# Scores of two heads issued in turn into two banks of one PSUM allocation, with the mixers' PSUM as two pairs of banks and one single

## The chip, the cores and the metric

One core of a Trainium2 chip runs the whole program. The metric is the device time of one execution in microseconds, the median of the runs. Lower is better.

## What is computed

One inference step of a two-layer encoder trunk for a prompt of 512 frames and 8 samples of 16 new frames each with 512 cached keys. The first layer mixes with stick-breaking attention (8 heads of 64) beside a gated linear attention (4 heads), the second with softmax attention (16 heads of 64); a SwiGLU feed-forward part follows each. Cut to what the change touches:

```python
# first mixer, attention: strictly causal, keys weighted by a running product
z = einsum('bthd,bshd->bhts', q, k) * 64 ** -0.5
log_keep = where(mask, log_sigmoid(-z), 0.0)
after = reverse cumulative sum of log_keep, without the key itself
o = einsum('bhts,bshd->bthd', where(mask, exp(log_sigmoid(z) + after), 0.0), v)
# second mixer: chunk band, learned bias on clipped relative distance
s = einsum('bthd,bshd->bhts', q, k) * 64 ** -0.5 + rel_table[:, rel]
o = einsum('bhts,bshd->bthd', softmax(where(mask, s, -inf)), v)
```

Outputs are the frames of prompt and samples, and the keys, values and states to be cached, all in float32.

## The kernel before

The kernel is written in a tile language. A scheduler puts each engine's instructions into one fixed order when the program is built, by priorities that the code sets and by its own model of durations; on the chip each engine works through its order, and an instruction waits until what it needs is there. `tile_pool(bufs=n)` is a pool of n buffers: a tile asked for under a tag waits until the last reader of an older tile of that buffer is done.

PSUM has eight banks. Three belong to `pp`, for the projections. The other five are handed out anew in each part: in the first mixer three to `za` and two to `zb`, in the second four and one (`BANKS`), in the feed-forward parts all five to one pool.

Prompt attention works on pairs of heads (p = 0 to 3 in the first mixer, 0 to 7 in the second), whose 64-wide queries and keys lie on partitions 0 to 63 and 64 to 127 of `qT` and `kT`, each as a high and a low part. `attend_prompt` (L426) goes over four blocks b of 128 queries; block b sees n = 128(b+1) keys. For each head it takes a bank `z` from `za`, issues three score matmuls (high by high, high by low, low by high: L436, L437, L438; with the mask of the first mixer a fourth, L440), turns the scores into weights (`stick_break` L400, `softmax` L414: reduction L418, negation L420, exponential L421, reciprocal L422, scaling L423), transposes these in 128-wide pieces into the same bank (L444) and copies them out as `wT` (ScalarE for head 0, L447; VectorE for head 1, L449). Then both heads' value matmuls (L455) go into the first head's bank, and one copy (L457) ends the block.

Around it the projections `proj_ws` (tiles pw, L288 to L290) and `proj_as2` (pm) run from `pp`; after each key projection `evac_k` transposes the keys in `zb` (ktp). The gated linear attention `b_mix` takes its tiles at, og, kv, kvs, at4 and ms from `zb`.

Sample attention (`attend_sample`, L473) handles one sample and eight heads at a time: 8 times in the first mixer, 16 in the second. A bank `z` from `za` holds the scores throughout. For each of four key blocks j the keys are loaded (kr), transposed into a bank kttp (L489; which pool is told by `KTA` and `KTC`, one letter for each j), copied to SBUF (kt; VectorE L492, ScalarE L494) and multiplied (L496). The scores are copied (zsb, L499), made into weights, transposed back into `z` (L508, L510), copied (wTs L509, wT4 L511) and multiplied by the values (L517); the result is copied, transposed and copied once more (L520, L521, L525). Beside the samples run the output projection of the prompt (`out_prompt`, po, L561 to L563) and at the end that of the samples (`out_sample`, ps).

On TensorE a matmul uses the whole array of 128 rows and 128 columns, or a part: the profile writes 64*128 for the scores (64 rows), 128*64 for the values and 128*32 for the samples' products.

Of the kernel before, what the change touches and what calls it, by code (L numbers as in the profile page):

```python
# [8 lines left out]
F32 = mybir.dt.float32  # L9
# [7 lines left out]
P = 128  # L17
# [3 lines left out]
SEQ = 512  # L21
# [25 lines left out]
BANKS = ((3, 2), (4, 1))  # L47
KTA = "bbbb"
KTC = "baba"
# [6 lines left out]
def kernel(  # L56
# [16 lines left out]
    @contextmanager  # L73
    def mixer_pools(na, nb):

        with tc.tile_pool(name="mix", bufs=1, reuse_waits="tile") as m:
            pools["stage"] = m
            with tc.tile_pool(name="pza", bufs=na, space=PSUM, reuse_waits="tile") as a:
                with tc.tile_pool(name="pzb", bufs=nb, space=PSUM, reuse_waits="tile") as b:
                    banks.update(za=a, zb=b)  # L80
                    yield

    @contextmanager
    def ffn_pools():
        with tc.tile_pool(name="ffn", bufs=1, reuse_waits="tile") as m:
            pools["stage"] = m
            with tc.tile_pool(name="pf", bufs=5, space=PSUM, reuse_waits="tile") as a:
                banks.update(za=a, zb=a)
                yield
# [25 lines left out]

    def za(shape, name="za"):
        return banks["za"].tile(shape, F32, tag="za", name=name)
# [308 lines left out]
    def attend_prompt(qT, kT, v, c0, odst, weights, mask):  # L426


        for b in range(4):
            n = (b + 1) * P  # L430
            bs = slice(b * P, n)
            wTs, zs = [], []
            for h in range(2):
                z = za([P, 512], "z")
                r = slice(64 * h, 64 * h + 64)
                MM(z[:, :n], lhsT=qT[r, 0, bs], rhs=kT[r, 0, :n], start=True, stop=False)  # L436
                MM(z[:, :n], lhsT=qT[r, 0, bs], rhs=kT[r, 1, :n], start=False, stop=False)  # L437
                MM(z[:, :n], lhsT=qT[r, 1, bs], rhs=kT[r, 0, :n], start=False, stop=not mask)  # L438
                if mask:
                    MM(z[:, bs], lhsT=identb, rhs=mask_a, start=False, stop=True)  # L440
                w = weights(h, n, z[:, :n])
                wT = vr_([P, b + 1, P], "wT")
                for j in range(b + 1):
                    nc.tensor.transpose(z[:, j * P:(j + 1) * P], w[:, j * P:(j + 1) * P], ident)  # L444
                zv = z[:, :n].rearrange("p (j t) -> p j t", t=P)
                if h == 0:
                    nc.scalar.copy(wT, zv)  # L447
                else:
                    nc.vector.tensor_copy(wT, zv)  # L449
                wTs.append(wT)  # L450
                zs.append(z)
# [21 lines left out]
    def attend_sample(ck, cv, b, cs, qbd, zn, vnew, weights, oS, kttp):  # L473
# [8 lines left out]
        z = za([P, 512], "zs")  # L482
        for j in range(4):
# [3 lines left out]
            tp = (zb if kttp[j] == "b" else za)([P, 4, P], "kttp")  # L487
# [82 lines left out]
    def out_sample(W, x4, gi, hT):  # L570
        ps = [za([P, 512], "ps"), zb([P, 512], "ps")]
# [180 lines left out]
    stack.enter_context(mixer_pools(*BANKS[0]))  # L752
# [60 lines left out]
    def a_sample():  # L813
        with priority(FIRST + 100000):
            zn = new_key_scores(qbd, kfs, msn)
        for b in range(DB):
            with priority(FIRST + 100000 + 1000 * (b + 1)):
                attend_sample(cache_a_k, cache_a_v, b, slice(0, 512), qbd, zn, vt4[:, :512],
                              lambda zs: stick_break(528, zs, zs), oS[:, :4, :], KTA)

# [51 lines left out]
    def b_mix(pr, X0):  # L872
# [47 lines left out]
        kv = [zb([P, 4, P], "kv") for _ in range(2)]  # L920
# [34 lines left out]
        for h in range(2):  # L955
# [4 lines left out]
            at = zb([P, 4, P], "at")  # L960
# [7 lines left out]
            og = zb([P, SEQ], "og")  # L968
# [79 lines left out]
    stack.enter_context(mixer_pools(*BANKS[1]))  # L1048
# [33 lines left out]
    def c_sample(half):  # L1082
# [11 lines left out]
        for b in range(DB):  # L1094
            with priority(p + 1000 * (b + 1)):
                attend_sample(cache_c_k, cache_c_v, b, cs, qbd[half], zn, vt4[:, cs],
                              lambda zs: softmax(528, zs, zs, bsam[:, ::-1]),
                              oS[:, 4 * half:4 * half + 4, :], KTC)
# [69 lines left out]
```

## Time and profile before

| | |
|---|---|
| median of 3 runs | 1821.37 us (1815.55 to 1822.59) |
| profiled execution | 1823.8 us, span 1822.1 us |
| mean granted TensorE clock | 0.969 |
| TensorE, VectorE, ScalarE busy | 1732.9, 1142.8, 833.8 us |
| prompt's scores, first mixer | L436 from 67.1 to 306.6 us |
| prompt's scores, second mixer | L436 from 954.6 to 1199.6 us |

The table of windows gives, for a stretch of the span, the busy time of each engine, the granted clock (1.00 is full speed) and the share of the DMA engines. A row of the timeline is one instruction, or several equal ones merged (x2): start in us, length in us from the first start to the last end, engine, line, operation, tiles, array part, size. Successive matmuls overlap in the pipeline, so that the price of one is the distance between starts, not its length. A row of groups has count, busy us, mean ns of one, and the idle time of the engine before them.

### The profile page before, as it was taken

The numbers are of one execution on the slowest core, as the hardware profiler recorded it, in microseconds if no ns is written. First come the engines' busy times: TensorE is split into PE (matmuls) and PEld (weight loads), VectorE is DVE, ScalarE is ACT, GpSimd is POOL, SyncE is SP. The second block draws the span as 40 slices with busy tenths as digits, with TensorE's granted clock in tenths as the row PEclk, the third lists the DMA queues.
The fourth block names the chain that finished last, engine by engine and source line by source line (L and its number), as shares of the span: only waits on it lengthen the run. The fifth ranks groups of instructions, "written<-read, shape, count | busy, mean of one in ns | idle before, by whom it ended". The sixth has DMA issues, their size and how long they took to land.

```text
span 1822.1 us, 31879 instructions
## 1 busy us (share of the span) xinstructions
PE 1732.9 (95%) x12504; PEld 1550.1 (85%) x12504; DVE 1142.8 (63%) x2285; ACT 833.8 (46%) x1837; POOL 327.7 (18%) x355
## 2 busy tenths in 40 slices
PE   8999998998899999999799999999878999999997
PEld 7898986976898989989698888888757989999896
DVE  5466576767964846747635554665658747658475
ACT  6453444556642534525424333444545525435253
POOL 2000000002513413222200000000104314133130
PEclk9998997998999999999799999999988999999999
DMA  5311222573222232221342223257862222312212
GB/s 141 94 56 47 66 83 95 179 255 105 70 93 70 75 100 63 100 74 66 110 128 77 80 89 95 85 178 263 278 214 65 81 81 72 103 58 93 93 59 81
DMA packets 157430, 192.10 MB, mean 105 GB/s; under 512 B 13232, under 2 KB 109504, under 8 KB 157280
## 3 DMA queue, kind: packets, MB, share of 16 engines
q1 hardware_dynamic: 153696, 178.40, 30.4%
q0 software_dynamic: 3584, 11.67, 2.0%
q8 instruction: 98, 1.61, 0.4%
q14 instruction: 52, 0.43, 0.1%
HBM read 175.75 MB, written 14.29 MB: 104 GB/s over the span
## 4 chain that ended last, share of the span: by engine, by line
PE 80%; DVE 12%; DMA 4%; ACT 2%; issue 2%; SPq 0%; DVEq 0%; ACTq 0%
PE pn L307 6%; PE pn L309 5%; PE pn L308 5%; PE pw L288 5%; PE pw L289 5%; PE pw L290 5%; DVE wl L274 4%; PE px L653 3%; PE px L654 3%; PE px L655 3%; PE z L455 3%; PE py L655 3%; DMA kr<-in_cache_c_k_dram 2%; PE pm L337 2%; PE py L653 2%; PE py L654 2%
## 5 line engine op out<-in xcount | busy, mean ns | idle before, releaser
L274 DVE TENSOR_TENSOR wl<-raw,wh 128x512 fp32r<-128x512 f32 (+1 forms) x350 | 279.3, 807 | 220.8 <-ACT wh L273 218.7
L273 ACT CAST wh<-raw 128x512 fp32r<-128x512 f32 (+1 forms) x350 | 215.4, 618 | 347.3 <-PE pn L309 162.6
L659 POOL TENSOR_TENSOR sw<-raw 128x512 f32<-128x512 f32 x88 | 121.6, 1386 | 498.9 <-DMA raw<-in_w_ffn_gate_dram 292.9
L273 ACT CAST wh<-sw 128x512 fp32r<-128x512 f32 x176 | 109.3, 621 | 177.8 <-PE px L654 78.2
L274 DVE TENSOR_TENSOR wl<-sw,wh 128x512 fp32r<-128x512 f32 x176 | 139.7, 798 | 60.3 <-ACT wh L273 49.1
L308 PE MATMUL pn<-wl,gT 128*128 128x512 f32 x440 | 172.7, 393 | 0.0
L309 PE MATMUL pn<-wh,gT 128*128 128x512 f32 x440 | 170.7, 392 | 0.0
L307 PE MATMUL pn<-wh,gT 128*128 128x512 f32 x440 | 168.8, 394 | 0.0
L655 PE MATMUL py<-xb,wl 128*128 128x320 f32 x352 | 113.1, 321 | 8.4 <-DVE wl L274 8.2
L653 PE MATMUL py<-xb,wh 128*128 128x320 f32 x352 | 111.4, 316 | 6.1 <-ACT wh L273 4.6
L654 PE MATMUL pq<-xt,wh 128*128 128x320 f32 x352 | 109.1, 310 | 2.9 <-DVE xt L613 2.7
L654 PE MATMUL px<-xt,wh 128*128 128x320 f32 x352 | 109.7, 312 | 1.6 <-DVE xt L613 1.6
L654 PE MATMUL py<-xb,wh 128*128 128x320 f32 x352 | 110.7, 314 | 0.0
L653 PE MATMUL px<-xt,wh 128*128 128x320 f32 x352 | 109.5, 311 | 0.0
L655 PE MATMUL px<-xt,wl 128*128 128x320 f32 x352 | 109.4, 311 | 0.0
L653 PE MATMUL pq<-xt,wh 128*128 128x320 f32 x352 | 109.1, 310 | 0.1
L655 PE MATMUL pq<-xt,wl 128*128 128x320 f32 x352 | 108.6, 309 | 0.0
L309 PEld LDWEIGHTS pn<-wh,gT 128*128 128x128 f32 x440 | 83.5, 190 | 17.4
L308 PEld LDWEIGHTS pn<-wl,gT 128*128 128x128 f32 x440 | 83.6, 190 | 17.2
L307 PEld LDWEIGHTS pn<-wh,gT 128*128 128x128 f32 x440 | 83.4, 190 | 16.8
L288 PE MATMUL pw<-hTa,wh 128*128 128x320 f32 (+1 forms) x272 | 89.5, 329 | 0.0
L290 PE MATMUL pw<-hTa,wl 128*128 128x320 f32 (+1 forms) x272 | 88.7, 326 | 0.0
(331 smaller groups left out, 4778.3 us busy)
## 6 DMA issues: line engine op xcount, KB each, us to landing
raw<-in_w_ffn_gate_dram SPq DMA_DIRECT2D x44, 512.0 KB, 4.1
raw<-in_w_ffn_up_dram SPq DMA_DIRECT2D x44, 512.0 KB, 3.7
raw<-in_w_ffn_down_dram SPq DMA_DIRECT2D x44, 512.0 KB, 3.3
kr<-in_cache_c_k_dram SPq DMA_DIRECT2D x64, 256.0 KB, 4.8
vr<-in_cache_c_v_dram SPq DMA_DIRECT2D x16, 1024.0 KB, 6.7
raw<-in_w_in_ab_dram SPq DMA_DIRECT2D x24, 512.0 KB, 3.8
raw<-in_w_qkv_c_dram SPq DMA_DIRECT2D x24, 512.0 KB, 3.8
vr<-in_cache_a_v_dram SPq DMA_DIRECT2D x8, 1024.0 KB, 5.5
```

Source lines behind the costliest of these rows:

```text
L273: nc.scalar.copy(H, rawv)
L274: nc.vector.tensor_sub(L, rawv, H.bitcast(F32))
L288: MM(ps[i], lhsT=H[:, k % 4, :], rhs=hT[k][:, 0, s], start=(k == 0), stop=False)
L289: MM(ps[i], lhsT=H[:, k % 4, :], rhs=hT[k][:, 1, s], start=False, stop=False)
L290: MM(ps[i], lhsT=L[:, k % 4, :], rhs=hT[k][:, 0, s], start=False, stop=(k == 7))
L307: MM(ps[b], lhsT=lhs[k][:, 0, bs], rhs=H, start=(k == 0), stop=False)
L308: MM(ps[b], lhsT=lhs[k][:, 0, bs], rhs=L, start=False, stop=False)
L309: MM(ps[b], lhsT=lhs[k][:, 1, bs], rhs=H, start=False, stop=(k == K - 1))
L653: MM(ps, lhsT=H[:, k, :], rhs=X[x][0][k], start=(first and k == 0), stop=False, **f)
L654: MM(ps, lhsT=H[:, k, :], rhs=X[x][1][k], start=False, stop=False, **f)
L655: MM(ps, lhsT=L[:, k, :], rhs=X[x][0][k], start=False, stop=(k == 3), **f)
L659: nc.gpsimd.tensor_tensor(t, a, b, op=op)
```

## The change

The five banks of both mixers become two allocations of two banks (`zz`) and one single bank (`zb`). In `attend_prompt` one `zz` serves both heads of a block, and the score matmuls of the two heads stand in turn: high by high of head 0, of head 1, high by low of head 0, and so on. In `attend_sample` the second bank of the sample's `zz` takes the transposed keys of j = 0 and 2, the single bank those of j = 1 and 3. In `b_mix`, kv takes one `zz` for its two tiles, and at and og share one. What asked for a single tile of `za` in a mixer (the norms' transposes) gets a whole `zz`. The feed-forward parts keep one pool of five.

```diff
-            with tc.tile_pool(name="pza", bufs=na, space=PSUM, reuse_waits="tile") as a:
-                with tc.tile_pool(name="pzb", bufs=nb, space=PSUM, reuse_waits="tile") as b:
-                    banks.update(za=a, zb=b)
+            with tc.tile_pool(name="pzz", bufs=2, space=PSUM, reuse_waits="tile") as a:
+                with tc.tile_pool(name="pzb", bufs=1, space=PSUM, reuse_waits="tile") as b:
+                    banks.clear()
+                    banks.update(zz=a, zb=b)
...
+    def zz(name="zz"):
+        t = banks["zz"].tile([P, 2, 512], F32, tag="zz", name=name)
+        return [t[:, 0, :], t[:, 1, :]]
...
-            wTs, zs = [], []
-            for h in range(2):
-                z = za([P, 512], "z")
-                r = slice(64 * h, 64 * h + 64)
-                MM(z[:, :n], lhsT=qT[r, 0, bs], rhs=kT[r, 0, :n], start=True, stop=False)
-                MM(z[:, :n], lhsT=qT[r, 0, bs], rhs=kT[r, 1, :n], start=False, stop=False)
-                MM(z[:, :n], lhsT=qT[r, 1, bs], rhs=kT[r, 0, :n], start=False, stop=not mask)
-                if mask:
+            zs, wTs = zz("z"), []
+
+            for i, j in ((0, 0), (0, 1), (1, 0)):
+                for h in range(2):
+                    r = slice(64 * h, 64 * h + 64)
+                    MM(zs[h][:, :n], lhsT=qT[r, i, bs], rhs=kT[r, j, :n], start=(i + j == 0),
+                       stop=(i == 1 and not mask))
+            if mask:
+                for z in zs:
                     MM(z[:, bs], lhsT=identb, rhs=mask_a, start=False, stop=True)
+            for h, z in enumerate(zs):
                 w = weights(h, n, z[:, :n])
...
-        z = za([P, 512], "zs")
+        z, z2 = zz("zs")
...
-            tp = (zb if kttp[j] == "b" else za)([P, 4, P], "kttp")
+            tp = zb([P, 4, P], "kttp") if j % 2 else z2.rearrange("p (a t) -> p a t", a=4)
...
-        ps = [za([P, 512], "ps"), zb([P, 512], "ps")]
+        ps = zz("ps")
...
-        kv = [zb([P, 4, P], "kv") for _ in range(2)]
+        kv = [z.rearrange("p (a t) -> p a t", a=4) for z in zz("kv")]
...
-            at = zb([P, 4, P], "at")
+            at, og = zz("at")
+            at = at.rearrange("p (a t) -> p a t", a=4)
...
-            og = zb([P, SEQ], "og")
```

The scheduler's order moves with it. Lines of the new kernel stand ten higher (scores L446, transposes L455, values L465, keys' transposes L499, samples' products L506 and L527). Three places on TensorE follow; a number behind a name tells tiles apart, and the first part of a pair's name is what is written.

First, scores in the second mixer, pair 6, block b = 1, head 1 of the old order (z_12173), with the projection of the next keys (pw0) around them:

```order
L436 MATMUL z_12173<-kTc_11975,qTc_11974 128x256
L437 MATMUL z_12173<-kTc_11975,qTc_11974 128x256
L455 MATMUL z_12124<-wT_12136,vc_9538 64x128
L444 MATMUL z_12139<-ident_67,s_12143 128x128
L438 MATMUL z_12173<-kTc_11975,qTc_11974 128x256
L288 MATMUL pw0_12358<-hTc4_9244,wh_12354 128x320
```

In the new order both heads' six score matmuls of that block are one row:

```order
L455 MATMUL z_12061<-ident_67,s_12079 128x128
L446 MATMUL z_12093<-kTc_11912,qTc_11911 128x256 x6
L465 MATMUL z_12061<-wT_12076,vc_9499 64x128
L465 MATMUL z_12061<-wT_12087,vc_9499 64x128
L446 MATMUL z_12129<-kTc_11912,qTc_11911 128x384 x6
```

The heads' separate visits with other work between them have become one visit of six.

Second, the last pair of the second mixer, from block b = 1 on, before (po is the output projection, kttp a sample's keys):

```order
L436 MATMUL z_12479<-kTc_12281,qTc_12280 128x256
L437 MATMUL z_12479<-kTc_12281,qTc_12280 128x256
L438 MATMUL z_12479<-kTc_12281,qTc_12280 128x256
L562 MATMUL po_14456<-wl_14461,oHL_12590 128x256
L563 MATMUL po_14456<-wh_14460,oHL_12594 128x256
L561 MATMUL po_14456<-wh_14464,oHL_12591 128x256
L562 MATMUL po_14456<-wl_14465,oHL_12591 128x256
L563 MATMUL po_14456<-wh_14464,oHL_12595 128x256
```

and now:

```order
L446 MATMUL z_12395<-kTc_12214,qTc_12213 128x256 x6
L465 MATMUL z_12363<-wT_12378,vc_9499 64x128
L465 MATMUL z_12363<-wT_12389,vc_9499 64x128
L446 MATMUL z_12431<-kTc_12214,qTc_12213 128x384 x6
L455 MATMUL z_12395<-ident_67,s_12402 128x128 x2
L455 MATMUL z_12395<-ident_67,s_12414 128x128 x2
L455 MATMUL z_12431<-ident_67,s_12438 128x128 x3
L465 MATMUL z_12395<-wT_12410,vc_9499 64x128
```

The output projection that stood between the blocks is gone from there; each block's scores, transposes and values follow each other directly.

Third, late samples of the second mixer. Before, three samples take turns (zs_13374, zs_13520 and zs_13622 are their score banks):

```order
L517 MATMUL zs_13374<-vt4c_9536,wT4_13441 32x128 x4
L496 MATMUL zs_13622<-kt_13643,qbdc_9540 32x128 x4
L496 MATMUL zs_13622<-kt_13656,qbdc_9540 32x128 x4
L489 MATMUL kttp_13664<-ident_67,kr_13662 128x128 x4
L489 MATMUL kttp_13727<-ident_67,kr_13725 128x128 x4
L521 MATMUL zs_13374<-ident_67,osb_13469 128x128
L508 MATMUL zs_13520<-ident_67,zsb_13573 128x128 x4
```

and now two:

```order
L499 MATMUL zs_13733<-ident_67,kr_13759 128x128 x4
L499 MATMUL kttp_13773<-ident_67,kr_13771 128x128 x4
L518 MATMUL zs_13633<-ident_67,zsb_13684 128x128 x4
L506 MATMUL zs_13733<-kt_13765,qbdc_9501 32x128 x4
L506 MATMUL zs_13733<-kt_13778,qbdc_9501 32x128 x4
L499 MATMUL kttp_13848<-ident_67,kr_13846 128x128 x4
L520 MATMUL zs_13633<-ident_67,wn_13694 128x128
```

A sample's keys are now transposed into its own second bank or the single one, and the sample after next begins when the older one of the two is done.

More of the change, by code (lines that the diff above doesn't have):

```diff
@@ L73, in mixer_pools @@
     @contextmanager
[L74 removed]
+    def mixer_pools():
         with tc.tile_pool(name="mix", bufs=1, reuse_waits="tile") as m:
             pools["stage"] = m
[L78 to L80 removed]
+            with tc.tile_pool(name="pzz", bufs=2, space=PSUM, reuse_waits="tile") as a:
+                with tc.tile_pool(name="pzb", bufs=1, space=PSUM, reuse_waits="tile") as b:
+                    banks.clear()
+                    banks.update(zz=a, zb=b)
                     yield
@@ L87, in ffn_pools @@
             with tc.tile_pool(name="pf", bufs=5, space=PSUM, reuse_waits="tile") as a:
-                banks.update(za=a, zb=a)
+                banks.clear()
+                banks.update(za=a)
                 yield
@@ L114, in pp @@
         return pps.tile(shape, F32, tag="pp", name=name)
+    def zz(name="zz"):
+        t = banks["zz"].tile([P, 2, 512], F32, tag="zz", name=name)
+        return [t[:, 0, :], t[:, 1, :]]
     def za(shape, name="za"):
+        if "za" not in banks:
+            n = 1
+            for d in shape[1:]:
+                n *= d
+            t = zz(name)[0][:, :n]
+            return t if len(shape) == 2 else t.rearrange("p (a b) -> p a b", a=shape[1])
         return banks["za"].tile(shape, F32, tag="za", name=name)
@@ L471, in new_key_scores, with attend_sample @@
         return zn
-    def attend_sample(ck, cv, b, cs, qbd, zn, vnew, weights, oS, kttp):
+    def attend_sample(ck, cv, b, cs, qbd, zn, vnew, weights, oS):
         def rows(src):
@@ L751 @@
     stack = ExitStack()
-    stack.enter_context(mixer_pools(*BANKS[0]))
+    stack.enter_context(mixer_pools())
     nc.scalar.preload_act_table_set(LOGSET)
@@ L818, in a_sample @@
                 attend_sample(cache_a_k, cache_a_v, b, slice(0, 512), qbd, zn, vt4[:, :512],
-                              lambda zs: stick_break(528, zs, zs), oS[:, :4, :], KTA)
+                              lambda zs: stick_break(528, zs, zs), oS[:, :4, :])
     def b_gates():
@@ L1045 @@
     hT = hT2
-    stack.enter_context(mixer_pools(*BANKS[1]))
+    stack.enter_context(mixer_pools())
     W = w_qkv_c[0]
@@ L1097, in c_sample @@
                               lambda zs: softmax(528, zs, zs, bsam[:, ::-1]),
-                              oS[:, 4 * half:4 * half + 4, :], KTC)
+                              oS[:, 4 * half:4 * half + 4, :])
     for half in range(2):
```

4 lines of the change are left out of this document (removed).

## The prediction

> **What bounds the kernel now.** I read the page's busy shares first, then the table of windows, then the timeline of TensorE where scores are issued, then the costs of the softmax and of a sample.
>
> ```profile
> PE 1732.9 (95%) x12504; PEld 1550.1 (85%) x12504; DVE 1142.8 (63%) x2285; ACT 833.8 (46%) x1837; POOL 327.7 (18%) x355
> PE 80%; DVE 12%; DMA 4%; ACT 2%; issue 2%; SPq 0%; DVEq 0%; ACTq 0%
> ```
>
> TensorE is busy for 95% of the span and holds 80% of the chain that ended last. The change touches only the two mixers, so their windows decide (length, then busy us of PE, PEld, DVE, ACT and POOL, granted clock, DMA share, GB/s):
>
> ```profile
> 90.00:120.00 30.00, 30.00 (x211) 26.85 (x209) 20.57 (x36) 19.76 (x42) 1.29 (x2) 1.00 0.22 65
> 300.00:330.00 30.00, 25.43 (x235) 20.14 (x234) 22.19 (x38) 11.36 (x24) 1.50 (x3) 0.77 0.46 148
> 990.00:1020.00 30.00, 30.00 (x198) 25.03 (x197) 15.81 (x52) 11.36 (x31) 1.29 (x2) 1.00 0.31 93
> 1140.00:1170.00 30.00, 30.00 (x197) 25.31 (x198) 18.79 (x58) 14.80 (x35) 1.49 (x3) 1.00 0.21 65
> 1290.00:1320.00 30.00, 24.66 (x433) 19.35 (x435) 20.75 (x64) 19.52 (x52) 3.91 (x14) 1.00 0.91 306
> ```
>
> While the prompt's heads are attended to (60 to 300 us in the first mixer, 950 to 1205 in the second) TensorE is never free: 30.00 of 30. What is saved of its time there comes off the end. In the sample phase (the last row) it has gaps, with VectorE and ScalarE each near 20 of 30: that phase is a chain.
>
> **Why a head's scores cost what they do.** Here TensorE leaves a projection (pw, whole array), does one head's three score matmuls on 64 rows (N = 512) and comes back:
>
> ```profile
> 1037.97 0.31 PE L288 MATMUL pw<-hTc,wh 128*128 128x320 f32 x1
> 1038.21 0.49 PE L436 MATMUL z<-kTc,qTc 64*128 64x512 f32 x1
> 1038.55 0.39 PE L437 MATMUL z<-kTc,qTc 64*128 64x512 f32 x1
> 1038.78 0.39 PE L438 MATMUL z<-kTc,qTc 64*128 64x512 f32 x1
> 1039.10 0.42 PE L289 MATMUL pw<-hTc,wh 128*128 128x320 f32 x1
> 1039.35 0.31 PE L290 MATMUL pw<-hTc,wl 128*128 128x320 f32 x1
> 1039.50 0.31 PE L288 MATMUL pw<-hTc,wh 128*128 128x320 f32 x1
> ```
>
> Read the starts. A projection matmul starts 0.15 after the one before (1039.35 to 1039.50). From 1037.97 to 1039.35 are 1.38 us; two projection steps are 0.30 of it, so the visit cost 1.08. A score step is 0.23 (1038.55 to 1038.78), three are 0.70. The other 0.38 is the change of the array's shape, there and back: each matmul after a change starts 0.09 to 0.10 late, and its successor 0.10 late again. The shorter blocks give the step:
>
> ```profile
> 1045.28 0.27 PE L437 MATMUL z<-kTc,qTc 64*128 64x128 f32 x1
> 1045.39 0.27 PE L438 MATMUL z<-kTc,qTc 64*128 64x128 f32 x1
> 1023.11 0.28 PE L437 MATMUL z<-kTc,qTc 64*128 64x256 f32 x1
> 1023.23 0.28 PE L438 MATMUL z<-kTc,qTc 64*128 64x256 f32 x1
> 1028.19 0.34 PE L437 MATMUL z<-kTc,qTc 64*128 64x384 f32 x1
> 1028.37 0.33 PE L438 MATMUL z<-kTc,qTc 64*128 64x384 f32 x1
> ```
>
> That is 0.11, 0.12 and 0.18 us for N = 128, 256 and 384.
>
> **What two heads in turn cost.** The scheduler already let two heads meet in a few places. At the start of the second mixer "x2" is one matmul on rows 0 to 63 and one on rows 64 to 127:
>
> ```profile
> 955.37 0.33 PE L437 MATMUL z<-kTc,qTc 64*128 64x128 f32 x2
> 955.54 0.28 PE L438 MATMUL z<-kTc,qTc 64*128 64x128 f32 x2
> 955.65 0.34 PE L437 MATMUL z<-kTc,qTc 64*128 64x256 f32 x2
> 955.82 0.29 PE L438 MATMUL z<-kTc,qTc 64*128 64x256 f32 x2
> 956.03 0.41 PE L289 MATMUL pw<-hTc,wh 128*128 128x320 f32 x1
> ```
>
> The pair at 955.82 covers 0.29 us from first start to last end; one such matmul alone covers 0.28 (1023.23). The two run side by side. The pair at 955.54 is followed by the next after 0.11, the price of one matmul alone.
>
> **The change part by part.**
>
> *Overlap.* Per pair of heads the second head's steps cost 3 x (0.11 + 0.12 + 0.18 + 0.23) = 1.92 us. Twelve pairs (four and eight) make 23 us; counted in the order, 19 of the 144 steps already meet their partner, at 0.11 about 2 us. Left: 21 us. For N = 384 and 512 no pair stands in this trace; the ends are none (a pair costs two steps: 12 x 3 x 0.41 = 15 us less) and full overlap. I take full, as the four pairs shown do.
>
> The Trainium skill, "TensorE: Matmul & The Clock Gate", Part 3, gives 3.07 times for four row tiles, not 4; by that 77% the 21 us would be 16. The rows above show a pair at one matmul's price, and no run here shows four row tiles; the sum stays with the rows.
>
> *Fewer changes of shape.* The order has 557 neighbours on TensorE of different array shape before and 415 after. At 0.38/2 = 0.19 each the 142 would be 27 us; where two small shapes stand side by side only the entry (0.10) is sure, 14. I take 0.15: 21 us.
>
> Together TensorE needs 42 us less, nearly all of it in the full stretches.
>
> *Two allocations instead of three or four banks, prompt.* A block of 128 queries now holds both banks until its values are copied out, and only two blocks are under way. As long as projections stand between, that costs nothing: they fill TensorE. In the new order they run out: ten blocks of the second mixer's last three pairs follow each other with nothing between (the order shown above for the last pair). There a block costs what the slowest of three takes. VectorE's rows, in the second mixer's window (count, mean ns):
>
> ```profile
> L418 DVE CUSTOM_DVE_ANT_0 s<-z,bias 128x128 f32<-128x128 f32 (+3 forms) x64 | 31.2, 490 | 20.2 <-PE z L438 19.2 <-issue 0.6
> L423 DVE TENSOR_SCALAR s<-s,tot 128x128 f32<-128x128 f32 (+3 forms) x64 | 24.5, 386 | 1.4
> L449 DVE COPY wT<-z 128x128 f32<-128x128 f32 (+3 forms) x32 | 15.7, 490 | 15.9 <-PE z L444 15.4
> L422 DVE RECIPROCAL tot<-tot 128x1 f32<-128x1 f32 x64 | 10.2, 160 | 14.8 <-ACT s L421 14.5
> L420 DVE TENSOR_SCALAR m<-m 128x1 f32<-128x1 f32 x64 | 9.5, 150 | 0.9
> L457 DVE COPY oTc<-z 128x128 f32<-128x128 f32 x32 | 9.3, 291 | 28.6 <-PE z L455 28.4
> L421 ACT ACTIVATE s<-s,m 128x128 f32<-128x128 f32 (+3 forms) x64 | 36.0, 562 | 68.5 <-DVE m L420 68.5
> ```
>
> VectorE: 2 x (0.49 + 0.39 + 0.16 + 0.15) + 0.49 + 0.29 = 3.2 us a block. TensorE: three score steps 0.5, five transposes 0.5, the values 0.6, four changes of shape 0.6: 2.2. The chain alone: scores 0.5, two reductions 1.0, one exponential 0.6, the small ones 0.3, scaling 0.4, transposes 0.5, copy 0.5, values 0.6, copy 0.3, some ten handovers at 0.1 (an estimate): about 6, so 3 with two under way and 6 with one. The stall is between 3.2 - 2.2 = 1.0 and 3.8 a block, 10 to 38 us for ten. I take 1.4, near the lower end, since two are under way: +14 us.
>
> *Two samples under way instead of three.* ScalarE's copy of the transposed weights stands once in each sample; the first and the last of seven:
>
> ```profile
> 1295.38 0.59 ACT L509 COPY wTs<-zs 128x512 f32<-128x512 f32 x1
> 1338.37 0.58 ACT L509 COPY wTs<-zs 128x512 f32<-128x512 f32 x1
> ```
>
> and the longest steps of a sample's chain (count, mean ns):
>
> ```profile
> L494 ACT COPY kt<-kttp 128x512 f32<-128x512 f32 x31 | 18.2, 588 | 27.1 <-PE kttp L489 25.6 <-PE zs L496 1.4
> L421 ACT ACTIVATE zsb<-zsb,m 128x528 f32<-128x528 f32 x16 | 11.8, 736 | 9.7 <-DVE m L420 9.7
> L418 DVE CUSTOM_DVE_ANT_0 zsb<-zsb,bsam 128x528 f32<-128x528 f32 x16 | 11.3, 706 | 10.4 <-ACT zsb L499 10.0 <-issue 0.5
> L499 ACT COPY zsb<-zs 128x512 f32<-128x512 f32 x16 | 9.5, 591 | 7.0 <-PE zs L496 6.8
> L423 DVE TENSOR_SCALAR zsb<-zsb,tot 128x528 f32<-128x528 f32 x16 | 7.9, 493 | 0.4
> ```
>
> The copies give (1338.37 - 1295.38) / 6 = 7.2 us a sample, three under way, so a life of 21.5. TensorE's own part is 22 transposes at 0.11, 72 short matmuls of which four run in 0.11, and six changes of shape: 5.3. While the output projection (po) fills the gaps the period costs nothing. Its rows end after the 17th of the 24 samples in the old order and after the 14th in the new: seven uncovered samples become ten. A life without queueing: two rounds of transposes and copy 2.4, products 0.3, the five steps above less the first 2.5, the small ones 0.6, transposes and copies of the weights 1.8, values and output 2.3, some 16 handovers at 0.1: 11.5. With two under way the period is at best half of that, 6, and at worst 21.5 / 2 = 10.8. Old extra: 7 x (7.2 - 5.3) = 13. New: 10 x 0.7 = 7 to 10 x 5.5 = 55. I take a period of 7.5, near today's: 22, so +9 (ends -6 and +42).
>
> *The single bank and the first mixer's end.* Keys' transposes, the gate's products and the means share one bank instead of two; projections cover that (30.00 of 30 at 90:120). Were the cover gone, some 33 uses would wait about 0.5 each, 16 us. The end of the first mixer has no cover already: 300:330 loses 30 - 25.43 = 4.6 at a clock of 0.77. I put +2 between -4.6 and +4.6. Feed-forward parts keep their five banks; the start's transposes (ten tiles in two allocations, not three banks) are priced at nothing, hidden behind the loads of x.
>
> Sum: -21 - 21 + 14 + 9 + 2 = -17. The profiled execution took 1823.8 (span 1822.1 and 1.7 around it); that gives 1806.8. It lies 2.4 above the median of the runs, 1821.4: forecast 1805.
>
> **Rivals.**
>
> *A, the cover holds.* The prompt's blocks and the samples find work between after all, at the lower ends: -42 + 10 - 6 - 5 = -43, about 1779. For it: 30.00 of 30 in all attending windows. Against: the order itself, with ten uncovered blocks.
>
> *B, samples become the bound (other side).* One mechanism: with two under way a sample's life stays at 21.5 us, since the rows of a life are waits behind other samples' and the output projection's rows in VectorE's and ScalarE's queues. Then +42 in place of +9: -42 + 14 + 42 + 2 = +16, 1837. It is even from a period of 9.2 us on: 10 x (9.2 - 5.3) - 13 = 26. For it: VectorE 20.75 and ScalarE 19.52 of 30. Against: with three under way those queues are fuller than with two.
>
> *C, no overlap at N = 384 and 512.* 15 us less saved: -2, about 1819: no change. Nothing in the trace excludes it.
>
> *D, VectorE becomes the bound of the whole second mixer.* It is busy 18.79 of 30 at 1140:1170; TensorE's time there falls by some 29 in 250, to 26.5 of 30, still above. So VectorE binds only in the ten uncovered blocks, which the +14 holds. The Trainium skill, "TensorEngine Tiling (Array Packing)", Performance Considerations, warns that tiling speeds TensorE and leaves the emptying of PSUM as it was, which may then bind; by these rows that is so in the ten blocks alone, and the sum stands.
>
> **How the numbers follow.** Chances: forecast 0.52, A 0.18, B 0.15, C 0.10, the single bank's waits (+14 on the forecast, 1819) 0.05. The forecast's own range, from the ends of changes of shape (14 to 27) and of the uncovered blocks, is 1793 to 1820. For 8 in 10 the range takes half of A and part of B: 1781 to 1832. This kernel's runs tell 0.5% (9 us) from no change: 1812 and 1830 are the borders. Faster: most of the forecast (0.42) and A: 0.60. Same: the rest of the forecast, C and the bank: 0.24. Slower: B: 0.16.
>
> **What would show it.** Right: scores stand as x6, pairs within some ns; the 64-row matmuls' steps at N = 512 stay near 0.23 per pair; the second mixer's attending part shortens by 10 to 15 us, with TensorE under 30 of 30 only near its end; sample period 7 to 8 us. Wrong: pairs at N = 512 that take 0.46; a sample period over 9; granted clock below 1.00 before the last pairs.

## The result, and the profile after

The changed kernel takes 1885.84 us (median of 4 runs, 1882.82 to 1892.14) beside 1821.65 for the kernel before on the same chip (median of 4): 1.0364 times as long, 95% interval 1.0326 to 1.0402. The forecast was 1805 us, the range ended at 1832. The ratios of the later runs are to runs of the kernel before beside them, whose medians are 1817.4 to 1820.3. The profiled execution has a span of 1887.0 us (before 1822.1) and a mean granted clock of 0.943 (before 0.969).

Busy shares and the chain that ended last, from the page after:

```profile
PE 1723.5 (91%) x12504; PEld 1544.5 (82%) x12504; DVE 1157.8 (61%) x2285; ACT 835.7 (44%) x1837; POOL 328.4 (17%) x355
PE 76%; DVE 13%; ACT 4%; DMA 3%; issue 2%; DVEq 0%; ACTq 0%
```

TensorE is busy for 9 us less than before, in a span that is 65 us longer: it waits. The table of windows after, first the five stretches shown of before, then one from the end of the second mixer's attending:

```profile
90.00:120.00 30.00, 30.00 (x211) 26.70 (x210) 21.60 (x37) 22.98 (x47) 1.30 (x2) 1.00 0.21 65
300.00:330.00 30.00, 19.75 (x152) 13.66 (x152) 21.71 (x42) 12.78 (x31) 2.37 (x3) 0.56 0.34 112
990.00:1020.00 30.00, 29.05 (x203) 26.99 (x203) 15.88 (x53) 13.10 (x36) 2.23 (x5) 1.00 0.36 110
1140.00:1170.00 30.00, 27.37 (x193) 23.68 (x194) 16.47 (x57) 11.40 (x33) 1.69 (x4) 0.89 0.37 117
1290.00:1320.00 30.00, 26.57 (x318) 22.57 (x317) 15.24 (x45) 14.06 (x37) 3.86 (x11) 0.94 0.62 216
1230.00:1260.00 30.00, 24.16 (x177) 16.62 (x174) 15.32 (x48) 9.93 (x22) 0.20 (x1) 0.61 0.26 78
```

The busy column after the length is TensorE's. It was 30.00 at 1140:1170 before and is 27.37, and the clock falls below 1.00: 0.89 there, 0.61 at 1230:1260, 0.56 at 300:330 (0.77 before).

The two heads do run side by side. Timeline of TensorE after, scores of the second mixer for N = 384 and N = 512 at full clock, then one block at the end of the attending:

```profile
1045.54 0.79 PE L446 MATMUL z<-kTc,qTc 64*128 64x384 f32 x6
1048.73 0.96 PE L446 MATMUL z<-kTc,qTc 64*128 64x512 f32 x6 [0.39 <-DVE oTc L467]
...
1180.38 0.79 PE L446 MATMUL z<-kTc,qTc 64*128 64x384 f32 x6 [0.67 <-DVE m L429]
1181.75 0.51 PE L455 MATMUL z<-ident,s 128*128 128x128 f32 x2 [0.58 <-DVE s L432]
...
1185.07 1.65 PE L446 MATMUL z<-kTc,qTc 64*128 64x512 f32 x6
1188.03 0.88 PE L455 MATMUL z<-ident,s 128*128 128x128 f32 x3 [1.32 <-DVE s L432]
1189.74 1.55 PE L465 MATMUL z<-wT,vc 128*64 128x128 f32 x12 [0.83 <-DVE wT L460]
...
1192.41 0.90 PE L446 MATMUL z<-kTc,qTc 64*128 64x128 f32 x6
1195.82 1.30 PE L455 MATMUL z<-ident,s 128*128 128x128 f32 x5 [2.51 <-DVE tot L431]
```

Six score matmuls at N = 512 take 0.96 us from first start to last end. Three of one head took as much before (1038.21 to 1038.78 + 0.39). At 1185.07 the same six take 1.65: the granted clock is 0.50 from 1184 to 1188. Scores of successive blocks start 4.7 and 7.3 us apart (1180.38, 1185.07, 1192.41), and in between TensorE waits for the softmax (the brackets above: idle time and what ended it).

For the comparisons I cut the profiled execution of each kernel into five parts: the first mixer (to the first matmul of its feed-forward part), from there to the first score of the second mixer, the second mixer's attending (to the end of the last copy oTc), its samples (to the first matmul of its feed-forward part), the rest. Times in us:

| kernel | median | first mixer | to 2nd mixer | attending | samples | rest |
|---|---|---|---|---|---|---|
| before | 1821.65 | 453.5 | 501.1 | 253.7 | 172.7 | 441.1 |
| changed | 1885.84 | 491.7 | 496.8 | 266.9 | 190.0 | 441.6 |
| e2 pools only | 1943.85 | 495.9 | 497.5 | 319.6 | 192.7 | 440.7 |
| e3 change in first mixer | 1853.35 | 490.8 | 496.0 | 253.7 | 168.4 | 440.2 |
| e5 samples as before | 1859.70 | 484.8 | 495.2 | 262.3 | 167.2 | 445.7 |
| e6 samples alone changed | 1868.53 | 481.5 | 494.8 | 251.7 | 199.5 | 441.3 |
| e9 two samples, single banks | 1848.41 | 477.5 | 496.4 | 251.1 | 181.1 | 439.3 |
| e17 short chain | 1866.91 | 468.6 | 497.0 | 266.8 | 190.9 | 440.6 |
| e7 at, og single | 1893.51 | 493.2 | 497.8 | 264.6 | 192.6 | 444.5 |
| e10 second attending changed | 1834.20 | 457.4 | 500.2 | 266.3 | 171.3 | 441.2 |
| e11 e10, output elsewhere | 1828.08 | 451.8 | 498.9 | 249.3 | 183.1 | 443.3 |
| e18 changed, output elsewhere | 1903.15 | 517.6 | 496.0 | 249.5 | 196.3 | 440.5 |
| e12 changed, filled | 1888.49 | 489.5 | 497.8 | 260.8 | 196.8 | 440.9 |
| e1 turn only | 1817.99 | 443.5 | 501.0 | 254.5 | 169.5 | 443.8 |
| e13 turn, output elsewhere | 1798.48 | 455.4 | 499.2 | 225.9 | 178.9 | 440.7 |
| e14 output elsewhere | 1792.80 | 454.6 | 498.7 | 221.5 | 170.2 | 443.0 |
| e19 e14 in both mixers | 1804.75 | 466.7 | 501.7 | 221.6 | 174.7 | 443.8 |

The changed kernel against before: first mixer +38, second mixer's attending +13, its samples +17, the stretch between -4. One execution of a kernel can differ from its median by some 5 us, so parts are read to about that; e1, as fast as the kernel before, is 10 us shorter in its first mixer.

Two stretches tell where the time of the attending went: from the start to the first mixer's last block (its last copy oT), and the second mixer's attending. Both rows of before, then both of after:

```profile
0.00:329.50 329.50, 315.31 (x2234) 275.84 (x2234) 203.35 (x422) 154.09 (x371) 22.10 (x54) 0.95 0.28 84
954.60:1208.30 253.70, 253.05 (x1819) 211.95 (x1819) 142.59 (x472) 97.79 (x260) 13.43 (x26) 1.00 0.28 87
```

```profile
0.00:351.60 351.60, 316.66 (x2250) 278.99 (x2251) 212.18 (x433) 156.93 (x378) 23.93 (x57) 0.89 0.27 80
988.50:1255.40 266.90, 240.29 (x1818) 206.13 (x1817) 143.07 (x473) 97.86 (x260) 13.24 (x26) 0.89 0.27 83
```

TensorE stands idle for 14 us of the first before and 35 after, for 1 and 27 us of the second. In the second its busy time falls by 13 us, at a clock of 0.89 instead of 1.00.

### The profile page after: what moved, and what is told of

The parts are those of the page before. It is cut to its first block, busy times and chain, and to the rows that moved or that the text cites. A ratio compares the mean times of both kernels' runs of the same rounds, so it can differ in the third digit from the quotient of the medians.

```text
span 1887.0 us, 31860 instructions
## 1 busy us (share of the span) xinstructions
PE 1723.5 (91%) x12504; PEld 1544.5 (82%) x12504; DVE 1157.8 (61%) x2285; ACT 835.7 (44%) x1837; POOL 328.4 (17%) x355
## 4 chain that ended last, share of the span: by engine, by line
PE 76%; DVE 13%; ACT 4%; DMA 3%; issue 2%; DVEq 0%; ACTq 0%
PE pn L316 5%; PE pn L317 5%; PE pn L318 5%; PE pw L297 4%; PE pw L298 4%; PE pw L299 4%; DVE wl L283 4%; PE px L663 3%; PE px L664 3%; PE px L665 3%; PE py L665 3%; PE py L664 2%; PE py L663 2%; PE pm L346 2%; PE pm L348 2%
## 5 line engine op out<-in xcount | busy, mean ns | idle before, releaser
L283 DVE TENSOR_TENSOR wl<-raw,wh 128x512 fp32r<-128x512 f32 (+1 forms) x350 | 284.6, 822 | 235.5 <-ACT wh L282 226.0
L297 PE MATMUL pw<-hTa,wh 128*128 128x320 f32 (+1 forms) x272 | 90.3, 332 | 2.0 <-DVE qT L375 1.4
L298 PE MATMUL pw<-hTa,wh 128*128 128x320 f32 (+1 forms) x272 | 89.1, 327 | 0.0
```

The lines of the kernel that those rows point to most:

```text
L283: nc.vector.tensor_sub(L, rawv, H.bitcast(F32))
L297: MM(ps[i], lhsT=H[:, k % 4, :], rhs=hT[k][:, 0, s], start=(k == 0), stop=False)
L298: MM(ps[i], lhsT=H[:, k % 4, :], rhs=hT[k][:, 1, s], start=False, stop=False)
```

## Experiments: which half of the change costs

My theory after the result: with two allocations held for a whole block or sample too little is under way, TensorE waits, and its clock falls; issue in turn is a gain. The rivals: issue in turn itself is the loss; only the samples, or only the first mixer's single bank, matter.

**e2, the pools alone.** The changed kernel with the old score loop:

```diff
-            for i, j in ((0, 0), (0, 1), (1, 0)):
-                for h in range(2):
...
+            for h, z in enumerate(zs):
+                r = slice(64 * h, 64 * h + 64)
+                MM(z[:, :n], lhsT=qT[r, 0, bs], rhs=kT[r, 0, :n], start=True, stop=False)
...
```

> The changed kernel's two pairs of banks and one single bank everywhere, but the two heads' scores one after the other as before. Theory 'few allocations' (two blocks or two samples under way leave TensorE waiting, and its granted clock falls with the gaps; issue in turn is itself a gain): slower still than the changed kernel, by the 15 to 25 us of overlap, about 1905 us (1890 to 1920). Rival 'in turn' (both heads' scores at once bunch the softmax of both heads behind them, and that made the loss): near the kernel before, 1815 to 1840 us. Rival 'order' (any other order of the scheduler costs this much, whatever the banks): about 1886, as the changed kernel.

1943.85 us, 1.0688 times the kernel before (1.0657 to 1.0720). The pools cost 125 us by themselves, and issue in turn gives 58 back. The rivals "in turn" and "order" are out. My own 1905 was missed too, by 39 us: issue in turn gives back more than the 15 to 25 I expected. Nearly all of it lies in the second mixer's attending, 319.6 to 266.9:

```profile
993.40:1313.00 319.60, 279.00 (x1818) 234.91 (x1817) 143.83 (x473) 98.20 (x260) 13.23 (x26) 0.83 0.22 69
```

Against the changed kernel's row above, TensorE is busy for 39 us more and idle for 14 us more, at a clock of 0.83 instead of 0.89.

**e3, the change in the first mixer only** (the second mixer with `BANKS[1]` and the old loop).

> The change in the first mixer only; the second keeps its four and one single banks and the heads one after the other. By the landmarks of the two traces the first mixer lost 38 us up to the start of its feed-forward part, which gave 4 back. Theory 'few allocations': about 1855 us (1848 to 1862), and the second mixer as long as before (254 us from first score to last copied block). Rival 'one bank in the first mixer' (the gated attention's tiles and the keys' transposes queue for one single bank and the pairs, and nearly all of the loss is there): 1870 us or more. Rival 'second mixer' (its samples with two under way are the loss): below 1840.

1853.35 us, 1.0193 (1.0158 to 1.0227): +35. The first mixer is 37 us longer, the second 4 us shorter than before. The rest of the 64, some 30, belongs to the second mixer by difference; the change was not run in that mixer alone.

**e5 and e6, attending and samples apart.** The five banks are handed out anew ahead of `mixer_end`: in e5 from pairs to the banks of before (shown for the first mixer), in e6 the other way round.

```diff
+    hand_out(*BANKS[0])
     xt = mixer_end(w_out_ab[0], oT, oS, lambda b: x_rows(x_prompt, xs_flat, b), 1, hT, a_sample,
```

> As the changed kernel up to the samples in both mixers; then the five banks are handed out anew for the samples and the outputs as in the kernel before (three and two in the first mixer, four and one in the second, with its letters for the transposed keys). By the landmarks the sample parts lost 19 and 20 us. Theory 'few allocations', both kinds of phase: about 1847 us (1838 to 1858), sample periods back at 10.3 and 8.7 us. Rival 'attending is the loss, the samples only follow it' (the samples' longer periods come from later work around them): above 1870. Rival 'samples are all of it': below 1830.

> As the kernel before up to the samples in both mixers (single banks, heads one after the other, no score in turn); then for the samples and the outputs two pairs and one single bank as in the changed kernel. Theory 'few allocations': 1822 + 39 = about 1861 us (1850 to 1870). Rival 'attending is the loss': within 10 us of the kernel before, 1815 to 1832. My prediction's term for this part alone was +9: 1831.

e5: 1859.70 us (1.0235, 1.0199 to 1.0272). e6: 1868.53 (1.0284, 1.0254 to 1.0313). Each half costs 40 to 50 us alone, together 64: in the first mixer +31 and +28 alone, +38 together; why the two do not add up there was not separated. e5 lies 2 us above its theory's range, e6 inside. In the second mixer the samples are the larger part: +27 alone (e6), while e5 is 3 us above before there, attending and samples together. "Either alone is the whole" is out in both directions.

**e9, two samples under way in single banks.** As before up to the samples, then two banks for scores and three for transposed keys (`hand_out(2, 3)`, `KTC = "bbbb"`).

> The kernel before up to the samples; then for the samples two single banks for scores and three for transposed keys, so that two samples are under way in single banks that come free one by one. Theory 'depth' (two under way is the loss, whatever the form of the allocation): as with pairs for the samples alone, 1868 within 8 us, sample periods of 14 and 10 us. Rival 'form' (the second bank bound to its sample and the one single bank shared by both is the loss): near the kernel before, 1820 to 1835.

1848.41 us (1.0139, 1.0104 to 1.0173), between what the theory and the rival say. The copies wTs, one a sample, give the periods. Rows of that tile (count, duration, first and last start) of before, of the changed kernel, of e9, and of e6, whose attending is that of before, as in e9:

```profile
L509 ACT COPY wTs<-zs x8: 566/587/589, 347.0 to 419.4; 128x512 f32<-128x512 f32 x8
L509 ACT COPY wTs<-zs x16: 577/587/592, 1217.2 to 1347.5; 128x512 f32<-128x512 f32 x16
```

```profile
L519 ACT COPY wTs<-zs x8: 576/586/587, 352.6 to 458.0; 128x512 f32<-128x512 f32 x8
L519 ACT COPY wTs<-zs x16: 575/585/587, 1264.4 to 1413.2; 128x512 f32<-128x512 f32 x16
```

```profile
L550 ACT COPY wTs<-zs x8: 565/586/587, 351.2 to 441.2; 128x512 f32<-128x512 f32 x8
L550 ACT COPY wTs<-zs x16: 576/585/592, 1241.4 to 1377.0; 128x512 f32<-128x512 f32 x16
```

```profile
L550 ACT COPY wTs<-zs x8: 567/586/588, 348.4 to 445.5; 128x512 f32<-128x512 f32 x8
L550 ACT COPY wTs<-zs x16: 579/586/596, 1241.5 to 1396.7; 128x512 f32<-128x512 f32 x16
```

In the first mixer a sample comes every (419.4 - 347.0) / 7 = 10.3 us before, 15.1 after, 12.9 in e9 and 13.9 in e6; in the second every 8.7, 9.9, 9.0 and 10.3. Compare e9 and e6 with before: in the first mixer most of the longer period (2.6 of 3.6 us) is that two are under way. In the second most (1.3 of 1.6) is the form: a second bank bound to its sample after its keys are done, and one single bank for the other keys. Which of these two costs it was not separated.

**e17, a shorter chain.** In the first mixer's samples the logarithm, maximum, running sum and subtraction are left out, so their outputs are no longer the attention's:

```diff
-                              lambda zs: stick_break(528, zs, zs), oS[:, :4, :])
+                              short, oS[:, :4, :])
...
+    def short(zs):
+        nc.scalar.activation(zs, zs, AF.Abs)
+        nc.scalar.activation(zs, zs, AF.Exp, scale=-1.0)
+        return zs
```

> The changed kernel, but the samples of the first mixer take exp(-abs(z)) for their weights: logarithm, maximum, running sum and subtraction are left out, 0.6 + 0.65 + 1.25 + 0.7 = 3.2 us of engine time a sample and two handovers, 4 to 5 us of its life. The samples' results change by that. Theory 'with two samples under way the period is half a life': 2 to 2.5 us off the period of 15.0, 7 x 2.25 + 4.5 = 20 us off the first mixer, about 1866. Rival 'the period is set by an engine or by loads' (VectorE has 18 to 22 of 30, ScalarE 13 to 19, the DMA share is below 0.7): 1881 or more.

1866.91 us, 19 below the changed kernel. Tile wTs of e17:

```profile
L519 ACT COPY wTs<-zs x8: 577/586/587, 338.9 to 431.1; 128x512 f32<-128x512 f32 x8
```

The period is (431.1 - 338.9) / 7 = 13.2 us, 1.9 below the changed kernel's 15.1: about half of the 4 to 5 us taken from the chain. That is what half a life would give, and not what a bound by an engine or by loads would. That the time also met the forecast of 1866 is partly luck: the last copy comes 27 us earlier, of which the seven periods are 13; the first copy is 14 us earlier (338.9 instead of 352.6), of which the shorter chain explains 4 to 5.

## Experiments: what in attending costs

**e7, at and og in the single bank** (the two lines of `b_mix` put back to `zb`).

> The changed kernel, but the gated attention's at and og take the single bank one after the other again instead of a pair. In the first mixer of the changed kernel the prompt's attending ended 18 to 22 us later, behind projections at half clock that follow a run of at and og matmuls (projection step 0.266 us instead of 0.147 near 187 us). Theory 'pairs are short' (at and og take a pair away from the prompt's blocks): the first mixer gets 10 to 20 us shorter, about 1870 us. Rival 'the single bank is short': longer by 5 to 20 us, about 1898. Rival 'neither, it is the blocks' own depth': 1886 within 6.

1893.51 us (1.0393, 1.0360 to 1.0426), 8 above the changed kernel. The prompt's last block ended at 325.5 us instead of 351.6, but the gated attention's last matmuls moved from 306 to 320 and the first mixer's end stayed (493.2 instead of 491.7). So at and og did hold up the prompt's blocks, but the theory's 10 to 20 us were not gained: in the single bank they are late themselves. Here the shortage of banks moved and did not go away.

**e10 and e11, the second mixer's attending alone.** e10 has pairs and scores in turn there, everything else as before. e11 sums a block's output elsewhere:

```diff
-            o = zs[0][:, :P]
+            o = zb([P, P], "o")
```

> First mixer as before. Second mixer: pairs of banks and scores in turn for attending, but each block's output is summed in the single bank instead of the first head's, so that a pair comes free when both heads' weights are copied out, before the value matmuls; samples with the banks of before. In the run with pairs for attending and the samples' old banks, the second mixer up to its feed-forward part took 429.5 us, against 426.4 before. Theory 'holding time': the value matmuls, their wait and the copy (about 1 to 1.5 us of some 6) are off the pair's life, ten uncovered blocks gain 1 us each and the clock stays higher: 415 us there, kernel about 1811. Rival 'VectorE binds the uncovered blocks' (3.2 us of it a block): no change, 1822 to 1828. Rival 'single bank': keys' transposes wait for outputs, 1835 or more.

> First mixer as before; second mixer with pairs of banks and scores in turn for attending, samples with the banks of before. The same with a block's output in the single bank took 249.2 us for the second mixer's attending. Theory 'holding to the end of the block': 262 us there as in the run that had it in both mixers, kernel about 1825 us. Rival 'banks that come and go together': 249 within 4 us, kernel 1815 to 1820.

e10: 1834.20 us (1.0086, 1.0060 to 1.0113). e11: 1828.08 (1.0048, 1.0031 to 1.0066). The second mixer's attending in one window, e10 and e11 (the row of before stands under the result):

```profile
957.60:1223.90 266.30, 236.70 (x1782) 203.86 (x1781) 142.51 (x470) 96.32 (x258) 13.25 (x26) 0.90 0.27 83
```

```profile
950.70:1200.00 249.30, 230.98 (x1702) 198.75 (x1701) 141.75 (x469) 96.72 (x258) 13.07 (x25) 0.97 0.28 86
```

With pairs (e10) TensorE is idle for 30 us of the attending, at a clock of 0.90; its 266.3 us fit the theory (262) and not the rival (249), though the kernel is 9 us above the 1825. A pair that comes free before the value matmuls (e11) gives 17 us: holding to the end of the block costs at most that, since e11's window also holds 80 matmuls fewer; TensorE's idle time falls by 11 us. e11's samples took 12 of the 17 us back, 183.1 against 171.3: their first transposes of keys start 5 us after the attending's end (1205) and stood 76 us ahead of it in e10 (1148 against 1223.9). So e11 missed the 1811 that I expected of it.

**e18, the same in the changed kernel, both mixers.**

> The changed kernel with one line else: a block's output is summed in the single bank in both mixers, so that a pair comes free when both heads' weights are copied out. Theory 'holding to the end of the block': first mixer's attending back to about 335 us from 351.6, second mixer's from 266.9 to 250; the samples still have two under way, so the kernel comes to 1886 - 15 - 12 = about 1859 (1850 to 1868). Rival 'banks that come and go together': 1875 to 1890. Rival 'single bank' (keys' transposes, gates and outputs queue for it): above 1890.

1903.15 us (1.0465, 1.0439 to 1.0491). The second mixer's attending is 249.5, as in e11; the first mixer became 26 us longer, and its last block ended at 362.4 us where I expected 335. What TensorE waited for longest at 60 to 520 us of e18 (us in all, times, longest):

```profile
PE zs L518 <- ACT zsb L420: 11.5, 3, 6.7
PE ktp L397 <- DVE sq L1008: 8.5, 2, 4.7
PE z L455 <- ACT l L420: 6.9, 3, 5.1
PE ms L1003 <- DVE sq L1008: 4.3, 2, 3.0
PE o L465 <- DVE kn L401: 4.2, 1, 4.2
```

Transposes of keys (ktp) wait for the reader of the gated attention's mean square (ms), the next mean square for the same reader, outputs (o) for the reader of a key transpose: 17 us of waits on the single bank. So the theory holds in the second mixer, and the first fits the rival "single bank", which also has the time (above 1890).

**e12, idle matmuls in the waits.** In the changed kernel, pairs 5 to 7 of the second mixer (`fill` is 2 there and 0 elsewhere):

```diff
                 w = weights(h, n, z[:, :n])
+                for i in range(fill):
+                    MM(z, lhsT=qT[:, 0, bs], rhs=kT[:, 0, :], start=True, stop=True)
```

> The changed kernel with 48 idle matmuls more: in the last three pairs of the second mixer two of 128x512 go into each head's bank after its reduction and before its transposes, where TensorE waits for the softmax. They compute nothing that is used. At full clock they are 48 x 0.23 = 11 us. In the changed kernel the clock is 0.50 to 0.60 at 1180 to 1200 and 1230 to 1250 us. Theory 'the clock falls because TensorE waits, and the low clock is a good part of the loss': with the waits filled the clock stays above 0.85 there and the time falls by 5 to 20 us, about 1874, though work was added. Rival 'the chain of one block is the bound, the clock only shows it': 1886 to 1890, the fillers hidden. Rival 'TensorE's own work is the bound': 1897 or more.

1888.49 us (1.0366, 1.0343 to 1.0390), the same as the changed kernel. Windows of e12, then two of the changed kernel beside 0.61 at 1230:1260 above:

```profile
1170.00:1200.00 30.00, 25.06 (x225) 15.65 (x224) 18.81 (x75) 12.00 (x36) 1.50 (x3) 0.94 0.18 55
1200.00:1230.00 30.00, 27.45 (x215) 22.35 (x214) 16.93 (x55) 10.38 (x25) 0.00 (x0) 1.00 0.16 54
1230.00:1260.00 30.00, 21.92 (x210) 15.76 (x211) 15.92 (x47) 10.88 (x24) 0.68 (x4) 1.00 0.34 104
```

```profile
1170.00:1200.00 30.00, 21.22 (x199) 14.74 (x197) 17.36 (x68) 12.00 (x35) 1.49 (x3) 0.70 0.18 55
1200.00:1230.00 30.00, 24.75 (x188) 21.63 (x189) 16.88 (x54) 10.47 (x25) 0.00 (x0) 0.84 0.15 53
```

The clock rose to 0.94 and 1.00 and the attending got 6 us shorter, with 11 us of matmuls added; the samples ended when they do in the changed kernel (last copies oSc at 1419 and 1420). So the low clock is a consequence of the waits, it is worth some us of attending at most, and it does not set the kernel's time: my theory's second half falls.

## Experiments: the other way, and a faster kernel

**e1, scores in turn with the banks of before.** Only the loop is rewritten; `zs = [za([P, 512], "z") for _ in range(2)]`.

> The kernel before with its single banks; only the code of the scores is written in turn (high by high of head 0, of head 1, ...). In the order that the scheduler makes of it the heads mostly stay apart, because the two banks come free at different times: 30 neighbours of the two heads against 233 in the changed kernel, 557 changes of array shape as before. Theory 'the pair allocation is what puts the heads side by side': no change, 1815 to 1826 us. Rival 'writing in turn is worth something or costs something by itself': outside of that.

1817.99 us, ratio 1.0003 (0.9983 to 1.0024). Without the joint allocation the order keeps the heads apart, and nothing changes.

**e13, e14 and e19, the output elsewhere with the banks of before.** e14 is the kernel before with `o = zs[0][:, :P]` turned into a tile of `zb` in the second mixer; e13 adds the loop of e1; e19 is e14 in both mixers.

> The banks of before (three and two, four and one), scores written in turn, and in the second mixer a block's output summed in the single bank, so that both heads' banks come free when their weights are copied out. The order now has 83 neighbours of the two heads and 484 changes of shape. The samples keep three and more under way. Theory 'holding time and depth are the loss, pairs and fewer changes the gain': the second mixer's attending (253.7 us before, TensorE busy all of it) gets shorter by 73 x 0.19 = 14 us for the changes and some 5 for pairs, and nothing is given back: 1805 us (1798 to 1812). Rival 'what attending gains the samples give back' (their loads and chains end when they end): 1815 to 1825. Rival 'the single bank is short': above 1825.

> The kernel before with one change: in the second mixer a block's output is summed in the single bank. Heads one after the other; the order has 472 changes of shape instead of 557 and 36 neighbours of the two heads. Theory 'changes of shape cost 0.19 us each': -16 us, about 1805. Rival 'the changes of shape that the order avoids lay beside waits': 1815 to 1825.

> The kernel before with the output of a block summed in the second pool's bank in both mixers (two banks there in the first mixer, one in the second). With it in the second mixer alone the kernel took 1793 us. Theory 'holding to the end of the block costs the first mixer too': attending there ends before 329.5 us, by up to 10, kernel 1783 to 1790. Rival 'the first mixer's attending is covered by projections': 1793 within 4. Rival 'the gated attention needs the two banks': 1798 or more.

e14: 1792.80 us, ratio 0.9858 (0.9833 to 0.9883). e13: 1798.48, 0.9891 (0.9865 to 0.9917). e19: 1804.75, 0.9931 (0.9907 to 0.9956). e14 beats both kernels. With the scores written in turn as well (e13), it is 6 us slower, at the fast end of what I expected of it. The second mixer's attending of e14 in one window:

```profile
953.30:1174.80 221.50, 219.61 (x1702) 194.19 (x1701) 132.88 (x469) 94.05 (x257) 13.73 (x25) 1.00 0.30 96
```

Against e11, where the output is in the same place, but the four banks are two pairs and the scores issued in turn, it is 28 us shorter with the same 1702 matmuls, although the two heads seldom meet (36 neighbours in its whole order). So in that mixer banks that come and go together cost more than the overlap brings. The gain over before, 32 us in attending, is more than the 16 I expected from 85 fewer changes of shape. Part of it is work moved: the window holds 117 fewer matmuls, and the samples after it are nevertheless 2.5 us shorter at a clock of 0.98 instead of 0.93. How the rest divides between changes of shape, earlier free banks and clock was not separated. e19 missed the 1783 to 1790 that I expected and shows the limit once more: its first mixer is 13 us longer than before. The prompt's last block ends 2 us earlier there (327.1 instead of 329.5), but the gated attention's last matmuls start at 310.5 instead of 302.9, and what follows takes 140 us instead of 124. That the gated attention lacks the second pool's banks is argued from these times, not tested alone.

## Why the prediction was wrong, step by step

- **Overlap, -21, and changes of shape, -21: right in sign, small in sum.** e2 against the changed kernel puts issue in turn at -58 against the -42. The six matmuls in 0.96 us show full overlap at N = 512, so rival C is out. Of the 58, 53 lie in the second mixer's attending: 39 of busy time and 14 of idle time. How the busy time divides between overlap, changes of shape and the higher clock was not measured.
- **Ten uncovered blocks, +14 (10 to 38): the mechanism was right, the term mis-sized.** TensorE waits there as forecast, but in the second mixer's attending it is idle for 27 us instead of 1, and its busy time falls by 13 us, not by the 28 of the 42 that belong to that mixer's eight pairs. So the stretch is 13 us longer: some 41 us against the forecast's saving. The step that failed is "a block costs what the slowest of three takes", taken near its lower end "since two are under way": the blocks shown came 4.7 and 7.3 us apart, not 3.2. A pair stays taken until the last copy (up to 17 us, e10 against e11), and its two banks come and go as one (28 us net of what issue in turn brings, e11 against e14). At a clock of 0.50 the six score matmuls take 1.65 us instead of 0.96.
- **Two samples under way, +9: failed.** I read the period from the second mixer alone and let it stand for all 24. The first mixer's copies in the same trace gave 10.3 us with three under way, a life of 31; half of it is 15.5, and 15.1 was measured. A life that stays as long with fewer under way is rival B's mechanism, in the mixer where I hadn't put it. The close agreement is partly luck: with two under way in single banks the period is 12.9 (e9), and the rest is the form of the banks. In the second mixer the period was 9.9, not 7.5, and the samples took 17 us more.
- **Single bank and first mixer's end, +2: failed, and the first mixer's attending had no term.** The first mixer was 38 us longer. Its attending alone costs 31 (e5), its samples alone 28 (e6). "As long as projections stand between, that costs nothing" and "projections cover that" were read from the order of before; with pairs the order itself changed: TensorE's idle time up to the prompt's last block rose from 14 to 35 us, and 300:330 fell from 25.43 busy to 19.75. Which of the shortages of banks there costs how much stays open; e7 moved it without removing it.
- **Clock: priced nowhere.** It fell as I had listed as a sign of being wrong; e12 shows that in the second mixer it followed the waits. In the first mixer's attending it was below 1.00 in places already before (0.87 at 150:180).
- **Rivals.** B had the sign, and half of the cause: the samples alone cost 50 us (e6), but the attending alone 41 (e5), and B's 1837 lacked that and the first mixer. D is refuted: VectorE has 15 to 17 of 30 in the uncovered stretch. A is out. Of the chances, the parts given for "same" and "slower" add up to 0.25 and 0.15, not 0.24 and 0.16, and TensorE was not quite "never free" in the first mixer's attending (29.48 of 30 at 270:300); neither changes the account.

The sum that came out: pools +125 (e2), issue in turn -58, together +67 (+64 measured side by side); the forecast had +25 and -42.

## What to carry to other kernels

A buffer's price here was how long it is held and with what it is tied, not only how many banks there are: in the second mixer's attending four banks as two pairs did 28 us worse than four single ones, although two matmuls at the price of one came with the pairs (e11 against e14). Ask of each accumulator which result keeps it taken longest; moving the small output of a block out of the score bank was worth 1.4% by one line (e14), and half of that in both mixers (e19). Read a chain's life in each stage where it runs, and divide it by what may be under way for a first, high estimate: it gave 15.5 for a measured 15.1 in the first mixer, but 13 (8.7 x 3 / 2) for a measured 9.9 in the second.

## What the hardware showed that I had not expected

The clock halved without TensorE standing idle. Timeline of the changed kernel in the first mixer:

```profile
183.91 0.66 PE L984 MATMUL at<-X,S 64*128 64x64 f32 x4
184.50 0.49 PE L980 MATMUL at<-am,vb 128*128 128x128 f32 x2
...
185.48 1.27 PE L974 MATMUL at<-X,X 64*128 64x128 f32 x5
186.68 0.63 PE L299 MATMUL pw<-hTa,wl 128*128 128x320 f32 x1
...
188.18 0.47 PE L298 MATMUL pw<-hTa,wh 128*128 128x320 f32 x1
188.45 0.47 PE L299 MATMUL pw<-hTa,wl 128*128 128x320 f32 x1
...
194.00 0.31 PE L297 MATMUL pw<-hTa,wh 128*128 128x320 f32 x1
194.15 0.31 PE L298 MATMUL pw<-hTa,wh 128*128 128x320 f32 x1
```

After some 4 us of small matmuls that change the array's shape (from 181.6), with no idle time between them in the timeline (where a matmul's end is modelled), projection steps are 0.27 us (188.18 to 188.45) and return to 0.15 by 194. The granted clock is 1.00 at 182 to 184 us, 0.50 at 186 to 192 and 1.00 again at 194. The kernel before shows such a fall too: TensorE is busy throughout 150 to 180 us, at a clock of 0.87.

```profile
150.00:180.00 30.00, 30.00 (x197) 26.49 (x196) 17.80 (x31) 10.41 (x19) 0.76 (x1) 0.87 0.19 53
```

The Trainium skill, "TensorE: Matmul & The Clock Gate", Part 1, puts the fall to half rate down to an idle window of about 3.4 us. Its two levels, full and half rate, agree with the granted clock here; but the rate fell with no such window, and in the second mixer it had fallen to 0.50 at 1182 us behind single waits of 0.8 us at most (0.67 and 0.58 in the rows at 1180.38 and 1181.75). It looks as if thin or interrupted work counted as idleness; no run here tests that.
